# Weights of the up projection in raw buffers only, and both weight layouts as parts of two tiles

## The chip, the core and the metric

The kernel runs on one core of one Trainium2 chip. Time is device time of one execution in microseconds (us), less is better; a figure for a kernel is the median of its runs. A core has five engines with instruction streams of their own: TensorE (PE in the profile, with its weight loads shown apart as PEld), VectorE (DVE), ScalarE (ACT), GpSimd (POOL) and SyncE (SP). Each works through its stream in order and waits on semaphores for the others. In this kernel SP issues the loads of weights, POOL issues most other transfers, and DVE and ACT prepare operands and move results out of the accumulators.

## What is computed

One layer of a decoder on 512 rows of width 2048, in 32-bit floats. Attention of two kinds comes first; the change touches the second half, a gated feed-forward block with a causal convolution of width 3:

```python
def conv_ffn(h, w_up, w_conv, b_conv, w_down):
    S = h.shape[1]
    u = h @ w_up
    up = jnp.pad(u, ((0, 0), (CONV_W - 1, 0), (0, 0)))
    conv = b_conv
    for j in range(CONV_W):
        conv = conv + w_conv[j] * up[:, j:j + S]
    gate, val = jnp.split(conv, 2, axis=-1)
    return (jax.nn.silu(gate) * val) @ w_down
...
        h = rms_norm(x, g_ffn[l]) * (1.0 + sc_f) + sh_f
        x = x + gt_f * conv_ffn(h, w_up[l], w_conv[l], b_conv[l], w_down[l])
```

`w_up` is 2048 x 11264 and `w_down` is 5632 x 2048. Both products take most of the second half of the time.

## The kernel before

**Exact products from split operands.** TensorE multiplies in a shorter format, so every operand is split: `hi` is the value rounded to that format (made by ACT, line 130) and `lo` is what is left (made by DVE, line 131, which needs `hi`). A product is three matmuls: hi by hi (line 1082), hi by lo (1083) and lo by hi (1084).

**Seven products in place of eight.** `seven` (line 947) multiplies a 2x2 block of weights by a 2x2 block of activations in the Strassen-Winograd way. A `Pair` is two blocks of 128 output columns. It has four weight blocks L11, L21, L22 and L12, and seven *steps*, in the order p1, p7, p6, p2, p5, p4, p3. Each step has a *preparation* (the function of that name: load blocks, add or subtract blocks on DVE in `comb`, split the result in `hilo`), then K x 3 matmuls of 256 columns, then an *evacuation* (e1 to e3: the bank is copied by ACT at line 987 or added to a slot by DVE at line 993). For the up projection K is 8, so a step has 24 matmuls and a pair 168; there are 40 pairs, 280 steps and 6,720 matmuls. The sums are

- p1: load L11 and L21; split L11
- p7: S3 = L21 - L11; split S3; load L22
- p6: L21 = L21 + L22, then L11 = L21 - L11; split L11; load L12
- p2: split L12
- p5: split L21; L12 = L12 - L11; L11 and L21 are free
- p4: split L22; L22 is free
- p3: split L12; L12 is free

`run` (line 1073) writes for step q first the preparation of step q + AHEAD (2 for the up projection, 3 for the down projection), then its matmuls, then its evacuation. A scheduler then orders each engine's stream by its own simulation of the program, so an instruction may stand earlier on its engine than it was written.

**Two kinds of storage.** *Raw buffers* hold loaded weights: five of 1104 floats per partition, taken from the left of the queue `rawq` and put back on its right. Three pairs of `hi_b`, `lo_b` hold the split weights and are used in turn (`cnt["wt"]` modulo 3), so the split for step q must wait until the matmuls of step q - 3 are done. *Slots* are 81 tiles of 512 floats for everything else: activations, sums, evacuated results. In the up projection `slots=True` (line 1534, the first 34 pairs) puts S3 and L12, 1024 floats each, into two slots each. Each operation on them is then two instructions of 512 columns (`cuts`, `part`), and the load of L12 is two transfers of 256 KB. The last six pairs use raw buffers for all blocks, in queue order: S3 then takes the *oldest* free raw buffer.

**The turn.** The down projection has blocks of 640 or 768 floats and other buffers: seven raw and four split pairs of 768. `weight_bufs` closes the pool of tiles and opens another in the same memory. `turn` does this, and writes the first three preparations of the down projection, behind the matmuls of the very last up step (line 1085).

**Around it.** After each pair of the up projection `ffn_out` does the convolution (ACT line 1379, DVE lines 1380 and 1381), the gate (ACT 1460, DVE 1463) and, in `f_out`, sums on DVE (1401 to 1404) and stores of the result to DRAM through POOL (1397, 1406). The down projection reads these back through POOL (`load_tile`, line 1482: two transfers, one for each half of a slot) and splits them (`split_tile`); `ahead` starts this in the last 56 up steps, as far as slots are free. Stores that add to the output run through POOL too (1553). Ahead of the 40 pairs, `up_group(0)` does the first 512 gate and value columns by plain products (`lin_fm`, splits at lines 122 and 123 in the same `hi_b`, `lo_b`).

Of the kernel before, what the change touches and what calls it, by code (L numbers as in the profile page):

```python
# [10 lines left out]
F32 = mybir.dt.float32  # L11
F32R = mybir.dt.float32r  # L12
# [6 lines left out]
P = 128  # L19
T = 512  # L20
# [11 lines left out]
def trunk_layer_kernel(  # L32
# [68 lines left out]
    weight_bufs(5, 3, 1104)  # L101
    ctx.callback(wpool.close)
    cnt = {"wt": 0, "half": 0, "at": 0}
# [165 lines left out]
    for ks in (range(0, 7), range(7, 14), range(14, KD)):  # L269
# [4 lines left out]
        for k in ks:  # L274
            t = get()
# [653 lines left out]
    class Pair:  # L929


        def __init__(self, rs, load, fin, K=KH, scale=None, slots=False):
            self.rs, self.load, self.fin, self.K, self.scale, self.slots = rs, load, fin, K, scale, slots

    def seven(work, pairs_of_banks, hook=None, AHEAD=2):
        def pair_steps(n, p):
# [18 lines left out]

            def part(t, lo, hi):

                for b, x, y in t:
                    if x <= lo and hi <= y:
                        return b[:, lo - x:hi - x]  # L960

            def cuts(*ts):
                return [(x, y) for _, x, y in max(ts, key=len)]

            def load(blk, slots=False):
                t = new(slots)
                for b, x, y in t:
                    SP.dma_start(b[:, :y - x], p.load(blk)[:, x:y])
                return t

            def hilo(t):
                i = cnt["wt"] % len(hi_b)
                cnt["wt"] += 1
                hi, lo = hi_b[i][:, :W], lo_b[i][:, :W]
                for x, y in cuts(t):
                    split(hi[:, x:y], lo[:, x:y], part(t, x, y))
                return hi, lo

            def comb(o, a, b, op):
                for x, y in cuts(o, a, b):  # L980
                    V.tensor_tensor(part(o, x, y), part(a, x, y), part(b, x, y), op)  # L981
# [18 lines left out]
            def p7():  # L1000
                s3 = new(p.slots)
                comb(s3, L[21], L[11], ALU.subtract)
                r = hilo(s3)
                done(s3)
                L[22] = load(3)
                return r

            def p6():
# [3 lines left out]
                L[12] = load(2, p.slots)  # L1012
# [56 lines left out]
        def start():  # L1069
            for q in range(AHEAD):  # L1070
                prepare(q)

        def run(then=None):
            for q, (_, o, r, ev, first, K) in enumerate(steps):
                prepare(q + AHEAD)
                wh, wl = ready.pop(q)
# [8 lines left out]
                if then and q == len(steps) - 1:  # L1085
                    then()
# [447 lines left out]
    work = [Pair(rs, lambda blk, i=i: w_ups[i, blk], ffn_out(i), slots=i < NF_ - 10) for i in range(NF_ - 4)]  # L1534
# [26 lines left out]
    up_start, up_run = seven(work, all_banks, up_hook)  # L1561
# [73 lines left out]
```

## Time and profile before

| | |
|---|---|
| median of three runs | 2711.05 us (2710.53, 2711.05, 2716.68) |
| the profiled execution | 2708.11 us, of which the span of its instructions is 2706.3 us |
| PE busy | 2613.8 us, 97% of the span, 17,200 matmuls |
| DVE, ACT, POOL busy | 2180.2 us (81%), 1281.9 us (47%), 363.6 us (13%) |
| moved | 464.33 MB, 172 GB/s on average |
| matmuls of lines 1082, 1083, 1084 | 3,920 each, 1108.2, 1101.6 and 1094.3 us busy |
| splits by line 130 (ACT) and 131 (DVE) of raw buffers | 458 each, 424.6 and 482.1 us busy |
| loads of `w_ups` | 126 of 512 KB into raw buffers, 68 of 256 KB into slots |

How to read it: consecutive matmuls overlap in the records (a matmul of 256 columns is shown with 0.28 us, and the next begins about 0.12 us after it), so how fast PE goes is read from the number of matmuls in a stretch of time, not from its busy share. A view by *windows* gives for each engine the busy time and, in brackets, the count of instructions in a stretch, and the clock granted to PE as a share of full speed. A view of *waits* says which engine and line waited for which, with total us, number of times and the longest. A line of the *timeline* is start, duration, engine, line, operation, destination and sources; in square brackets is the idle time of the engine just before it, and what ended it. SPq is the queue of transfers that SP issues.

### The profile page before, as it was taken

How to read it: one execution, taken by the hardware profiler on the slowest of the kernel's cores; microseconds unless marked ns; L12 is line 12 of the kernel's file. 1: busy time of each engine (PE TensorE's matmuls, PEld its weight loads, DVE VectorE, ACT ScalarE, POOL GpSimd, SP SyncE). 2: the span in 40 equal slices, each digit the busy share in tenths (PEclk: the TensorE clock that was granted, in tenths of full speed). 3: DMA queues.
4: the chain of work that ended last, by engine and by line, in shares of the span. 5: the costliest groups of instructions: out<-in, count | busy, mean ns of one | idle time of the engine just before them, and what ended most of it. 6: DMA issues, size and time to landing. Idle time of an engine off the chain costs nothing.

```text
span 2706.3 us, 45437 instructions
## 1 busy us (share of the span) xinstructions
PE 2613.8 (97%) x17200; PEld 2345.9 (87%) x17200; DVE 2180.2 (81%) x3669; ACT 1281.9 (47%) x2069; POOL 363.6 (13%) x663
## 2 busy tenths in 40 slices
PE   6999999999999999999999999999999999999999
PEld 5787687778997767788789999999999988899999
DVE  7977976688878667983778888888889888778777
ACT  4333434334444455322545555555555555545454
POOL 1001011110032222110100000000001032413120
PEclk8999899999999999999999999999999999999999
DMA  9953136665585588962333343334334456767563
GB/s 340 339 160 98 33 112 213 196 217 164 195 265 158 164 260 283 332 231 94 133 128 114 124 139 115 127 114 141 127 110 148 131 178 181 188 163 192 138 204 116
DMA packets 220559, 464.33 MB, mean 172 GB/s; under 512 B 24330, under 2 KB 65700, under 8 KB 220340
## 3 DMA queue, kind: packets, MB, share of 16 engines
q1 hardware_dynamic: 175156, 344.93, 39.0%
q0 software_dynamic: 45152, 116.50, 15.0%
q8 instruction: 134, 2.20, 0.3%
q14 instruction: 85, 0.70, 0.1%
q10 hardware_dynamic: 32, 0.01, 0.0%
HBM read 397.11 MB, written 64.23 MB: 170 GB/s over the span
## 4 chain that ended last, share of the span: by engine, by line
PE 53%; DVE 16%; issue 15%; DMA 13%; POOL 2%; ACT 1%; SPq 0%; DVEq 0%; POOLq 0%; ACTq 0%
PE bank L134 9%; PE bank L135 9%; PE bank L136 9%; PE bank L1082 7%; PE bank L1083 7%; PE bank L1084 7%; DVE wlo L131 6%; DMA raw<-in_w_ups 5%; DMA slot<-in_w_ada 2%; DMA raw<-in_w_down 2%; DVE raw L981 2%; DVE slot L981 1%; DVE slot L1380 1%; DMA raw<-in_w_in 1%; DVE slot L1381 1%
## 5 line engine op out<-in xcount | busy, mean ns | idle before, releaser
L1082 PE MATMUL bank<-slot,whi 128*128 128x256 f32 x3920 | 1108.2, 283 | 44.8 <-DVE slot L991 13.1
L1083 PE MATMUL bank<-slot,whi 128*128 128x256 f32 x3920 | 1101.6, 282 | 0.4 <-DVE slot L131 0.4
L1084 PE MATMUL bank<-slot,wlo 128*128 128x256 f32 x3920 | 1094.3, 282 | 5.7 <-DVE wlo L131 5.6
L1082 PEld LDWEIGHTS bank<-slot,whi 128*128 128x128 f32 x3920 | 743.2, 190 | 58.3 <-DVE slot L993 16.5
L1084 PEld LDWEIGHTS bank<-slot,wlo 128*128 128x128 f32 x3920 | 737.2, 189 | 8.6 <-DVE wlo L131 8.3
L1083 PEld LDWEIGHTS bank<-slot,whi 128*128 128x128 f32 x3920 | 742.2, 189 | 0.9 <-DVE slot L131 0.6
L130 ACT ACTIVATE whi<-raw 128x1024 fp32r<-128x1024 f32 (+2 forms) x458 | 424.6, 928 | 463.8 <-PE bank L1083 352.0
L131 DVE TENSOR_TENSOR wlo<-raw,whi 128x1024 fp32r<-128x1024 f32 (+2 forms) x458 | 482.1, 1058 | 54.3 <-ACT whi L130 53.0
L122 ACT ACTIVATE whi<-raw 128x1024 fp32r<-128x1024 f32 (+4 forms) x182 | 187.2, 1031 | 392.0 <-PE bank L136 198.9
L123 DVE TENSOR_TENSOR wlo<-raw,whi 128x1024 fp32r<-128x1024 f32 (+4 forms) x182 | 216.5, 1191 | 147.7 <-ACT whi L122 146.3
L981 DVE TENSOR_TENSOR raw<-raw,raw 128x1024 f32<-128x1024 f32 (+2 forms) x252 | 265.2, 1053 | 68.7 <-DMA raw<-in_w_down 47.5
L135 PE MATMUL bank<-wlo,slot 128*128 128x512 f32 (+2 forms) x768 | 297.0, 387 | 0.9 <-DVE wlo L123 0.9
L134 PE MATMUL bank<-whi,slot 128*128 128x512 f32 (+2 forms) x768 | 289.6, 390 | 6.8 <-ACT slot L401 4.3
L136 PE MATMUL bank<-whi,slot 128*128 128x512 f32 (+2 forms) x768 | 292.0, 384 | 0.0
L135 PE MATMUL bank<-slot,whi 128*128 128x512 f32 (+1 forms) x656 | 263.0, 401 | 1.2 <-DVE slot L703 1.1
L134 PE MATMUL bank<-slot,whi 128*128 128x512 f32 (+1 forms) x656 | 260.8, 403 | 3.1 <-ACT slot L1370 2.3
L136 PE MATMUL bank<-slot,wlo 128*128 128x512 f32 (+1 forms) x656 | 257.5, 401 | 0.4 <-DVE wlo L123 0.4
L134 PEld LDWEIGHTS bank<-whi,slot 128*128 128x128 f32 x768 | 145.8, 190 | 38.1 <-ACT slot L401 4.4
L135 PEld LDWEIGHTS bank<-wlo,slot 128*128 128x128 f32 x768 | 146.2, 190 | 29.4 <-DVE wlo L123 1.4
L739 DVE SCALAR_TENSOR_TENSOR slot<-slot,c_act,slot 128x512 f32<-128x512 f32 x203 | 149.6, 749 | 25.3 <-DMA slot<-in_w_ada 24.3
L136 PEld LDWEIGHTS bank<-whi,slot 128*128 128x128 f32 x768 | 144.7, 189 | 28.4 <-issue 0.3
L130 ACT ACTIVATE whi<-slot 128x512 fp32r<-128x512 f32 x204 | 128.0, 628 | 82.0 <-PE bank L1083 60.7
(294 smaller groups left out, 3115.0 us busy)
## 6 DMA issues: line engine op xcount, KB each, us to landing
slot<-in_w_ada SPq DMA_DIRECT2D x344, 256.0 KB, 5.6
raw<-in_w_ups SPq DMA_DIRECT2D x126, 512.0 KB, 4.3
raw<-in_w_in SPq DMA_DIRECT2D x50, 512.0 KB, 3.6
raw<-in_w_down SPq DMA_DIRECT2D x64, 384.0 KB, 5.1
raw<-in_w_down SPq DMA_DIRECT2D x64, 320.0 KB, 4.2
slot<-f POOLq DMA_DIRECT2D x154, 128.0 KB, 3.8
slot<-in_w_ups SPq DMA_DIRECT2D x68, 256.0 KB, 2.7
f<-slot POOLq DMA_DIRECT2D x66, 256.0 KB, 5.3
```

The lines of the kernel that those rows point to most:

```text
L122: A.activation(hi, raw[:, :w], AF.Copy)
L123: V.tensor_tensor(lo, raw[:, :w], r32(hi), ALU.subtract)
L130: A.activation(dst_hi, src, AF.Copy)
L131: V.tensor_tensor(dst_lo, src, r32(dst_hi), ALU.subtract)
L134: PE.matmul(o, lh, rh, start=first, stop=False)
L135: PE.matmul(o, lh, rl, start=False, stop=False)
L136: PE.matmul(o, ll, rh, start=False, stop=last)
L739: V.scalar_tensor_tensor(acc, ts[i], c_act[:, k:k + 1], acc, op0=ALU.mult, op1=ALU.add)
L981: V.tensor_tensor(part(o, x, y), part(a, x, y), part(b, x, y), op)
L1082: PE.matmul(o, wh[:, ks], rh, start=first and k == 0, stop=False, skip_group_check=True)
L1083: PE.matmul(o, wh[:, ks], rl, start=False, stop=False, skip_group_check=True)
L1084: PE.matmul(o, wl[:, ks], rh, start=False, stop=last, skip_group_check=True)
```

## The change

The whole diff is below. It makes one tile `wraw` of 5 x 1104 floats and one tile `whl` of 6 x 1104; `weight_bufs` now only cuts them anew, and hands out the raw parts in the order in which the parts of the old layout that they overlap come free. The option `slots` and the helpers for blocks in two pieces go away: all 40 pairs of the up projection hold L11, L21, L22 and L12 in raw buffers. S3 takes the newest free raw buffer (`rawq.pop()`) and gives it back at once, and L22 and L12 take the oldest. `turn` is called in every step with the number of steps left: two steps ahead of the end it cuts the buffers anew and prepares the first down step, in the last step the second, and the third follows behind the up projection. `cnt["wt"]` is set to 2 ahead of the up projection, so that the split pair 0 is the one due at the new cut.

```diff
     bank = [psum.tile([P, T], F32, name=f"bank{i}") for i in range(8)]
-    wpool = ExitStack()
-    hi_b, lo_b, rawq = [], [], deque()
+    WR, WS = 5 * 1104, 6 * 1104
+    wraw = pool.tile([P, WR], F32, name="raw")
+    whl = pool.tile([P, WS], F32R, name="whl")
+    hi_b, lo_b, rawq, raw_at = [], [], deque(), []
+    cnt = {"wt": 0, "half": 0, "at": 0}
 
     def weight_bufs(nr, nh, w):
 
-        wpool.close()
-        wp = wpool.enter_context(tc.tile_pool(name=f"w{w}", bufs=1))
+
+        assert nr * w <= WR and 2 * nh * w <= WS and len(rawq) == len(raw_at)
+        age = [[i for i, t in enumerate(rawq) if t is b[0]][0] for b in raw_at]
+
+        def freed(x):
+            return max([a for a, (_, lo, hi) in zip(age, raw_at) if lo < x + w and x < hi], default=0)
+
+        raw_at[:] = [(wraw[:, i * w:(i + 1) * w], i * w, (i + 1) * w) for i in sorted(range(nr), key=lambda i: freed(i * w))]
         rawq.clear()
-        rawq.extend([wp.tile([P, w], F32, name=f"raw{w}_{i}") for i in range(nr)])
-        hi_b[:] = [wp.tile([P, w], F32R, name=f"whi{w}_{i}") for i in range(nh)]
-        lo_b[:] = [wp.tile([P, w], F32R, name=f"wlo{w}_{i}") for i in range(nh)]
+        rawq.extend(b[0] for b in raw_at)
+        hi_b[:] = [whl[:, 2 * i * w:(2 * i + 1) * w] for i in range(nh)]
+        lo_b[:] = [whl[:, (2 * i + 1) * w:(2 * i + 2) * w] for i in range(nh)]
+        cnt["wt"] = 0
 
     weight_bufs(5, 3, 1104)
-    ctx.callback(wpool.close)
-    cnt = {"wt": 0, "half": 0, "at": 0}
...
-            def new(slots=False):
-                if slots:
-                    return [(get(), 0, T), (get(), T, W)]
-                return [(rawq.popleft(), 0, W)]
-
             def done(t):
-                if len(t) == 1:
-                    rawq.append(t[0][0])
-                else:
-                    put(*(x[0] for x in t))
-
-            def part(t, lo, hi):
-
-                for b, x, y in t:
-                    if x <= lo and hi <= y:
-                        return b[:, lo - x:hi - x]
-
-            def cuts(*ts):
-                return [(x, y) for _, x, y in max(ts, key=len)]
-
-            def load(blk, slots=False):
-                t = new(slots)
-                for b, x, y in t:
-                    SP.dma_start(b[:, :y - x], p.load(blk)[:, x:y])
+                rawq.append(t)
+
+            def load(blk):
+                t = rawq.popleft()
+                SP.dma_start(t[:, :W], p.load(blk))
                 return t
 
             def hilo(t):
                 i = cnt["wt"] % len(hi_b)
                 cnt["wt"] += 1
                 hi, lo = hi_b[i][:, :W], lo_b[i][:, :W]
-                for x, y in cuts(t):
-                    split(hi[:, x:y], lo[:, x:y], part(t, x, y))
+                split(hi, lo, t[:, :W])
                 return hi, lo
 
             def comb(o, a, b, op):
-                for x, y in cuts(o, a, b):
-                    V.tensor_tensor(part(o, x, y), part(a, x, y), part(b, x, y), op)
+                V.tensor_tensor(o[:, :W], a[:, :W], b[:, :W], op)
...
             def p7():
-                s3 = new(p.slots)
+
+                s3 = rawq.pop()
                 comb(s3, L[21], L[11], ALU.subtract)
                 r = hilo(s3)
                 done(s3)
...
-                L[12] = load(2, p.slots)
+                L[12] = load(2)
                 return r
...
-        def start():
-            for q in range(AHEAD):
+        def start(*qs):
+            for q in qs or range(AHEAD):
                 prepare(q)
 
         def run(then=None):
             for q, (_, o, r, ev, first, K) in enumerate(steps):
                 prepare(q + AHEAD)
+                if then:
+                    then(q - len(steps))
                 wh, wl = ready.pop(q)
...
-                if then and q == len(steps) - 1:
-                    then()
                 ev()
...
-    work = [Pair(rs, lambda blk, i=i: w_ups[i, blk], ffn_out(i), slots=i < NF_ - 10) for i in range(NF_ - 4)]
+    work_up = [Pair(rs, lambda blk, i=i: w_ups[i, blk], ffn_out(i)) for i in range(NF_ - 4)]
...
-    def turn():
-        weight_bufs(7, 4, 768)
-        down_start()
-
+    def turn(q):
+
+
+        if q == -2:
+            assert cnt["wt"] % 3 == 0
+            weight_bufs(7, 4, 768)
+        if q >= -2:
+            down_start(q + 2)
+
+    cnt["wt"] = 3 - len(work_up) * 7 % 3
     up_start()
     up_run(turn)
+    down_start(2)
     down_run()
```

More of the change, by code (lines that the diff above doesn't have):

```diff
@@ L929, in trunk_layer_kernel, with __init__ @@
     class Pair:
-        def __init__(self, rs, load, fin, K=KH, scale=None, slots=False):
-            self.rs, self.load, self.fin, self.K, self.scale, self.slots = rs, load, fin, K, scale, slots
+        def __init__(self, rs, load, fin, K=KH, scale=None):
+            self.rs, self.load, self.fin, self.K, self.scale = rs, load, fin, K, scale
     def seven(work, pairs_of_banks, hook=None, AHEAD=2):
@@ L1559, in down_pair @@
                     scale=tuple(mod[:, 80 + n:81 + n] for n in ns))
-    up_start, up_run = seven(work, all_banks, up_hook)
+    up_start, up_run = seven(work_up, all_banks, up_hook)
     work = [down_pair(c, j) for c in range(len(DH)) for j in range(KD // 2)]
```

## The prediction, made before the changed kernel was run

> **What bounds the kernel now.** I read the page first, then windows along the up projection, then who waits for whom in two stretches of it, then the timeline of one pair and of the turn.
>
> ```profile
> span 2706.3 us, 45437 instructions
> PE 2613.8 (97%) x17200; PEld 2345.9 (87%) x17200; DVE 2180.2 (81%) x3669; ACT 1281.9 (47%) x2069; POOL 363.6 (13%) x663
> PE 53%; DVE 16%; issue 15%; DMA 13%; POOL 2%; ACT 1%; SPq 0%; DVEq 0%; POOLq 0%; ACTq 0%
> ```
>
> PE is busy 97% of the span, yet only 53% of the chain of waits is PE. Since matmuls overlap in the records, the busy share hides small gaps, so I count matmuls in windows.
>
> ```profile
> core 0: us, PE busy (x) PEld busy (x) DVE busy (x) ACT busy (x) POOL busy (x), PEclk, DMA share, GB/s
> 1402.50:1500.00 97.50, 93.45 (x784) 92.59 (x783) 88.71 (x132) 51.05 (x79) 8.64 (x16) 1.00 0.39 136
> 1500.00:2083.00 583.00, 572.22 (x4782) 566.33 (x4782) 514.43 (x741) 311.83 (x485) 35.53 (x66) 1.00 0.38 128
> 2083.00:2200.00 117.00, 116.68 (x988) 116.48 (x988) 104.95 (x128) 63.20 (x86) 8.62 (x16) 1.00 0.41 128
> ...
> 2223.00:2227.00 4.00, 0.00 (x0) 0.00 (x0) 1.28 (x2) 0.69 (x2) 2.64 (x5) 0.65 0.95 305
> 2227.00:2231.00 4.00, 3.83 (x16) 3.54 (x17) 3.92 (x7) 2.56 (x5) 0.53 (x1) 0.50 0.87 328
> 2231.00:2240.00 9.00, 6.42 (x47) 5.60 (x47) 9.00 (x15) 6.81 (x12) 5.86 (x12) 1.00 0.72 221
> ```
>
> The matmuls of the pairs begin at 1402.5. Until 2083 the pairs hold S3 and L12 in slots; from 2083 to 2200 run the last six, which hold all in raw buffers. So this trace has both schemes in it. A matmul takes 583/4782 = 0.1219 us in the first stretch and 117/988 = 0.1184 us in the second. PE's best 50 us show what is left after that:
>
> ```profile
> 2150.00:2200.00 50.00, 50.00 (x426) 50.00 (x425) 43.54 (x52) 26.52 (x35) 3.77 (x7) 1.00 0.47 148
> ```
>
> 50/426 = 0.1174 us. Who waits, in the stretch with slots (DVE's and PE's waits, two answers), and then in the stretch without:
>
> ```profile
> DVE slot L981 <- DMA raw<-in_w_ups: 55.4, 27, 4.2
> DVE raw L981 <- DMA raw<-in_w_ups: 5.4, 15, 0.8
> ...
> PE bank L1082 <- DVE slot L993: 7.6, 19, 0.8
> PE bank L1084 <- DVE wlo L131: 2.8, 3, 1.3
> ```
>
> ```profile
> DVE raw L981 <- DMA raw<-in_w_ups: 7.3, 9, 2.1
> ...
> PE bank L1082 <- DVE slot L993: 0.3, 1, 0.3
> ```
>
> With slots, DVE stands 55.4 us at S3 (line 981 into a slot) for a load, in order, and behind it stand the additions of line 993 that empty a bank that PE wants to write. One such case:
>
> ```profile
> 1869.61 1.23 DVE L981 TENSOR_TENSOR raw<-raw,raw 128x1024 f32<-128x1024 f32 x1 [0.81 <-DMA raw<-in_w_ups]
> 1870.75 0.69 DVE L131 TENSOR_TENSOR wlo<-slot,whi 128x512 fp32r<-128x512 f32 x1
> 1871.36 0.42 DVE L993 TENSOR_TENSOR slot<-bank,slot 128x256 f32<-128x256 f32 x1
> ...
> 1871.83 0.39 PE L1082 MATMUL bank<-slot,whi 128*128 128x256 f32 x1 [0.49 <-DVE slot L993]
> ```
>
> **The change part by part.** *Blocks in raw buffers.* Per slot pair, S3 (one sum, one split) and L12 (one sum, two splits) lose two-piece form: five DVE and three ACT operations go from two instructions to one.
>
> ```profile
> L131 DVE TENSOR_TENSOR wlo<-raw,whi 128x1024 fp32r<-128x1024 f32 x114 | 139.1, 1220 | 1.7 <-ACT whi L130 1.0 <-PE bank L1083 0.7
> L131 DVE TENSOR_TENSOR wlo<-slot,whi 128x512 fp32r<-128x512 f32 x172 | 117.8, 685 | 0.3 <-ACT whi L130 0.3
> L981 DVE TENSOR_TENSOR slot<-raw,raw 128x512 f32<-128x512 f32 x56 | 36.3, 689 | 55.4 <-DMA raw<-in_w_ups 55.4
> ```
>
> By these durations each merge saves 2 x 685 - 1220 = 150 ns. But instructions overlap: the row at 1870.75 is followed after 0.61 us though it lasts 0.69, and the one at 1869.61 after 1.14 though it lasts 1.23. So a merge is worth 2 x 0.61 - 1.14 = 0.08 us, 0.4 us of DVE a pair of 20.5 us. (The Trainium skill, VectorE: DVE Perf Modes, The DRAIN you can't avoid, says that the next operation does not start until the pipe is empty, save one that is not held; by the first the merge would be worth the full 0.15 us. The starts above, 0.08 us ahead of the end, decide for the second.) DVE is not what sets the end here, so this alone I cost at nothing on PE; the waits matter.
>
> The load of L12 becomes one transfer of 512 KB for two of 256 KB: the same bytes, one issue fewer on SP, which has only these loads. When can the loads start? In the changed order L11 takes the buffer that S3 of the last pair had (free early), L21 the one freed by p5's subtraction, L22 the one freed by p5's split, L12 the one freed by p4's split. S3 needs L21 and the buffer that p3's split has just left. In one pair of the trace:
>
> ```profile
> 1844.48 0.69 DVE L981 TENSOR_TENSOR slot<-slot,raw 128x512 f32<-128x512 f32 x1
> 1845.09 1.22 DVE L131 TENSOR_TENSOR wlo<-raw,whi 128x1024 fp32r<-128x1024 f32 x1
> ...
> 1847.29 1.22 DVE L131 TENSOR_TENSOR wlo<-raw,whi 128x1024 fp32r<-128x1024 f32 x1
> ...
> 1850.81 0.68 DVE L131 TENSOR_TENSOR wlo<-slot,whi 128x512 fp32r<-128x512 f32 x1
> 1852.67 1.29 DVE L981 TENSOR_TENSOR slot<-raw,raw 128x512 f32<-128x512 f32 x2 [1.18 <-DMA raw<-in_w_ups]
> ```
>
> ```profile
> raw<-in_w_ups SPq DMA_DIRECT2D x84, 512.0 KB, 4.7
> ...
> DMA to landing us min/median/max: 2.5/3.6/7.5
> ```
>
> p5's subtraction ends at 1845.2, so L21 lands at 1849.9 by the median 4.7 of this stretch. p3's split ends at 1851.5, so S3 would wait for DVE's own work and not for the load, with 1.6 us to spare. L22 (from 1846.3) is wanted only after S3, L12 (from 1848.5) three steps on. Today the scheduler puts S3 a pair early, because its slots are free, and there it meets a load that has just been issued. So I take the rate of the last six pairs: 4782 x 0.1184 = 566.3, a gain of 16.7 us; bounds: half of it (8), and PE's best rate, 583 - 4782 x 0.1174 = 21.6.
>
> *The first pairs and the reset of the counter.* 784 matmuls in 97.5 us could be done in 92.8, but part of the 4.7 us lies in the start, where DVE and ACT still work off the plain products. 182 splits at line 122 and 56 of the gate's pairs have been counted by then, so the next split pair would be 238 mod 3 = 1; the change sets it to 2. p1 then waits for the last plain group but one, and p7's split for the last group, at 1402.7.
>
> ```profile
> 1402.74 1.06 ACT L130 ACTIVATE whi<-raw 128x1024 fp32r<-128x1024 f32 x1 [0.41 <-PE bank L135]
> ...
> 1404.53 1.22 DVE L131 TENSOR_TENSOR wlo<-raw,whi 128x1024 fp32r<-128x1024 f32 x1
> ```
>
> p7 gets the place that p6's split has here and is done at 1405.7; PE wants it after 24 matmuls, at 1402.7 + 2.8 = 1405.5. So 0.2 us, at most a split (1.1 + 1.2). Net gain of this part 1 us, bounds -2 and 4.7. In the last six pairs only the choice of buffers changes: 0, at best 117 - 988 x 0.1174 = 1.
>
> *The turn.* Now the first down load waits until the last up matmul has read its weights:
>
> ```profile
> 2221.51 27.23 SPq L968 DMA_DIRECT2D raw<-in_w_down  x11
> ...
> 2226.31 0.74 ACT L130 ACTIVATE whi<-raw 128x640 fp32r<-128x640 f32 x1 [3.57 <-DMA raw<-in_w_down]
> ...
> 2227.10 0.58 PE L1082 MATMUL bank<-slot,whi 128*128 128x256 f32 x1 [5.62 <-ACT whi L130]
> ```
>
> After the change the first loads wait for raw parts that are free steps earlier, and the first two splits for split pairs 0 and 1, read last by the third and second step from the end: 2 x 2.8 and 2.8 us ahead of the end. So the wait of 5.62 us goes. But from 2227 to 2240 DVE is busy 3.92 of 4 and 9.00 of 9 us (splits of what the down projection reads back, and the last convolution), and PE does 63 matmuls where 111 fit. This stall is next in line: DVE's work is not less, it only begins sooner, so the gain is DVE's idle time in the hole, 4 - 1.28 = 2.7 us, and some tenths around it. I take 3.3; bounds 0 (the loads meet POOL's at 0.95 of the DMA engines) and 5.6 + 2.1 = 7.7, which adds the half clock of 2227 to 2231, where 16 matmuls did what 34 could. The clock fell to 0.65 and 0.50 behind the hole and was 1.00 after 2231. (The Trainium skill, TensorE: Matmul & The Clock Gate, The HAM clock gate, has an idle window of about 3.4 us halve the clock; the trace agrees, and by this rule a hole under 3.4 us would keep full clock, and the sum would be 2.1 us better if DVE let PE use it.)
>
> The seven down buffers and four split pairs are as large as before; after the turn I expect the same, at 0.
>
> **Sum**, against the profiled execution: 2708.1 - 16.7 - 1.0 - 0 - 3.3 = 2687.1. The median of the runs is 2.9 above that execution, so 2690.
>
> **The rivals.** *Half:* PE waits for line 993 because DVE is full (514 of 583 us), not because of the loads; then 8 of the 16.7 and 2 at the turn: 2701. Against it: the last six pairs have DVE just as full (105 of 117 us) and PE waits 0.3 us. *All of it:* 21.6 + 2 + 1 + 7.7 = 32.3, so 2679; DVE's full stretch at the turn speaks against. *Given back:* PE reaches the down projection earlier, but what it reads back through POOL does not come earlier, and the down phase stretches to the old end, 2709. For it: POOL's loads are on the path after the turn. Against: what frees slots for them are up steps, which move too. *Slower, late loads:* five raw buffers with none to spare. At S3 DVE now stands 55.4 us in 28 pairs, 2.0 a pair. With 6.3 us between p5's subtraction and S3, a landing beyond 6.3 + 2.0 = 8.3 us makes it worse; at 9.3 in every pair, 40 x 1.0 = 40 us, some 2748. The longest landing in the stretch is 7.5, so it needs loads that delay each other. *Not what it says:* if parts of one tile were ordered like the whole, each load would wait for all readers, 4.7 us exposed in some 160 loads, beyond 3000 us. Against it, halves of one slot are loaded back to back, half a microsecond apart, though a landing takes 2.4 to 3.8:
>
> ```profile
> 2202.42 1.59 POOL L1482 DMA_DIRECT2D slot<-f  x3
> ...
> DMA to landing us min/median/max: 2.4/3.1/3.8
> ```
>
> **How the numbers follow.** Forecast 0.60, half 0.17, all of it 0.07, given back 0.05, late loads 0.08, one tile 0.03. About 0.3% (8 us, below 2703) can be told from no change. Faster: 0.60 + 0.07 + 0.11 of the half case = 0.78; same: 0.06 of it + 0.05 = 0.11; slower 0.08 + 0.03 = 0.11. The range runs from 2678, just beyond all of it, to 2706, which takes in the half case and leaves out giving back and slower, 0.16.
>
> **What would show it.** Right: no line 981 into a slot; DVE's waits for the loads of the up projection at some 10 us for its whole length; 0.1184 us a matmul from start to end; the first load of the down projection before the last up matmul, no hole above 2 us there, the clock at 1.00, and DVE still full for 10 us. Wrong: new waits of line 981 for loads in raw buffers; the same rate with fewer DVE waits (half); or a slower down projection.

## The result and the profile after

The changed kernel takes 2672.2 us (median of 4 runs, 2669.1 to 2673.3) where the kernel before took 2713.9 us beside it (4 runs, 2710.5 to 2719.0): ratio 0.9843, 95% interval 0.9823 to 0.9863. The direction was forecast; the gain is about twice the forecast, and 2672.2 lies below the range of 2678 to 2706.

The page of the changed kernel: its span, the engines, the group of the sums (busy us, mean ns, idle us before them and what ended most of it), and the loads of the up projection (count, size, median us from issue to landing):

```profile
span 2670.9 us, 45030 instructions
PE 2610.9 (98%) x17200; PEld 2351.5 (88%) x17200; DVE 2178.5 (82%) x3499; ACT 1268.3 (47%) x1967; POOL 362.3 (14%) x663
...
L968 DVE TENSOR_TENSOR raw<-raw 128x1024 f32<-128x1024 f32 (+2 forms) x320 | 347.1, 1085 | 6.3 <-DMA raw<-in_w_ups 3.4
...
raw<-in_w_ups SPq DMA_DIRECT2D x160, 512.0 KB, 4.9
```

DVE has 170 instructions less and about the same busy time (2178.5 against 2180.2 us). The merging was costed at nothing on PE and at 0.4 us of DVE a pair, 13.6 us in 34 pairs; DVE's busy time in the first 34 pairs fell by only 1.9 us (619.9 to 618.0). The sums wait 3.4 us in all for loads of the up projection. The line numbers have moved. The matmuls are lines 1072 to 1074 now, the splits 138 (ACT) and 139 (DVE), the sums 968, the evacuations 974 and 972 (ACT) and 980 and 978 (DVE), the loads 957.

To see where the time went, I cut each trace at matmuls. Of the 11,760 matmuls of the three lines, in order of their starts, the first 1,344 belong to attention, the next 5,712 to the first 34 pairs, 1,008 to the last six, and 3,696 to the down projection. Each entry is the difference of two starts, in us:

| | span | start of the pairs | first 34 pairs | last six | turn | down projection |
|---|---|---|---|---|---|---|
| before | 2706.3 | 1402.7 | 698.1 | 120.4 | 5.9 | 474.8 |
| after | 2670.9 | 1406.0 | 679.4 | 125.0 | 0.1 | 455.8 |
| difference | -35.4 | +3.3 | -18.7 | +4.6 | -5.8 | -18.9 |

The rest of the difference, 0.1, is rounding and what follows the last matmul. The +3.3 can't be put down to the change: in the other kernels below the pairs start anywhere from 1400.5 to 1409.2. Nor is it shown to be no part of it. The 1,344 matmuls of attention are eight pairs that go through `seven` and `p7` too, so the change touches them as well: S3 takes the newest buffer there. From the first to the last of them it is 170.2 us before and 174.8 after; the four kernels here with the oldest buffer in these pairs have 170.2 to 172.7, the eleven with the newest 172.3 to 174.8.

Windows of the changed kernel (columns as before): the middle of the first 34 pairs, the last six, and the turn.

```profile
core 0: us, PE busy (x) PEld busy (x) DVE busy (x) ACT busy (x) POOL busy (x), PEclk, DMA share, GB/s
...
1500.00:1750.00 250.00, 250.00 (x2113) 250.00 (x2112) 226.52 (x264) 132.60 (x176) 13.47 (x25) 1.00 0.39 131
...
2085.00:2210.00 125.00, 120.34 (x1010) 119.53 (x1008) 111.77 (x138) 68.62 (x98) 24.03 (x45) 1.00 0.47 153
2210.00:2214.00 4.00, 4.00 (x36) 3.95 (x34) 4.00 (x8) 3.52 (x7) 3.42 (x7) 1.00 0.89 263
2214.00:2220.00 6.00, 3.32 (x24) 2.76 (x23) 6.00 (x10) 4.44 (x8) 2.66 (x6) 1.00 0.86 279
2220.00:2230.00 10.00, 8.44 (x69) 8.03 (x69) 10.00 (x20) 6.22 (x11) 4.92 (x9) 1.00 0.60 204
```

250/2113 is 0.1183 us a matmul, the forecast rate. At the turn there is no hole and the clock stays at 1.00, but DVE is full from 2210 to 2230 and PE does 129 matmuls where 169 would fit: the stall that was named as next in line is there. The transfers of SP at the turn begin 20 us ahead of the last up matmul (2210.4):

```profile
2190.31 45.75 SPq L957 DMA_DIRECT2D raw<-in_w_down  x14
```

The surprise is the down projection. Its waits in the kernel before (us in all, times, longest; DVE's, then PE's), from 2227 to 2702:

```profile
DVE raw L981 <- DMA raw<-in_w_down: 47.5, 26, 3.9
...
PE bank L1082 <- DVE slot L991: 13.1, 9, 3.1
```

and in the changed one, from 2210 to 2666:

```profile
DVE whl L139 <- ACT whl L138: 55.1, 64, 2.2
...
PE bank L1072 <- ACT slot L972: 5.5, 9, 1.3
PE bank L1074 <- DVE whl L139: 2.7, 4, 0.9
PE bank L1072 <- ACT whl L138: 2.3, 3, 1.6
```

DVE's 47.5 us of waits for loads are gone, and with them PE's 13.1 us for DVE's evacuations. One of those places in the kernel before:

```profile
2384.09 2.82 DVE L131 TENSOR_TENSOR wlo<-raw,whi 128x768 fp32r<-128x768 f32 x3
2389.19 0.96 DVE L981 TENSOR_TENSOR raw<-raw,raw 128x768 f32<-128x768 f32 x1 [2.29 <-DMA raw<-in_w_down]
2390.07 0.48 DVE L991 SCALAR_TENSOR_TENSOR slot<-bank,mod,slot 128x256 f32<-128x256 f32 x1
...
2390.60 0.38 PE L1082 MATMUL bank<-slot,whi 128*128 128x256 f32 x1 [0.99 <-DVE slot L991]
```

This is the picture that the prediction drew for the slots of the up projection, in the down projection, which has no slots: a sum waits for a load, the evacuation queues behind it, PE waits for the bank.

### The profile page after: what moved, and what is told of

Its sections match the earlier page's. It is cut to its first block, busy times and chain, and to the rows that moved or that the text cites. A ratio compares the mean times of both kernels' runs of the same rounds, so it can differ in the third digit from the quotient of the medians.

```text
span 2670.9 us, 45030 instructions
## 1 busy us (share of the span) xinstructions
PE 2610.9 (98%) x17200; PEld 2351.5 (88%) x17200; DVE 2178.5 (82%) x3499; ACT 1268.3 (47%) x1967; POOL 362.3 (14%) x663
## 5 line engine op out<-in xcount | busy, mean ns | idle before, releaser
L1072 PE MATMUL bank<-slot,whl 128*128 128x256 f32 x3920 | 1104.2, 283 | 20.5 <-ACT slot L972 5.5
L1073 PE MATMUL bank<-slot,whl 128*128 128x256 f32 x3920 | 1099.9, 282 | 0.2 <-DVE slot L139 0.2
L1074 PE MATMUL bank<-slot,whl 128*128 128x256 f32 x3920 | 1088.0, 281 | 6.3 <-DVE whl L139 6.3
L138 ACT ACTIVATE whl<-raw 128x1024 fp32r<-128x1024 f32 (+2 forms) x560 | 532.7, 953 | 617.2 <-PE bank L1073 404.3
L1072 PEld LDWEIGHTS bank<-slot,whl 128*128 128x128 f32 x3920 | 739.6, 189 | 27.7 <-ACT slot L972 8.2
L1073 PEld LDWEIGHTS bank<-slot,whl 128*128 128x128 f32 x3920 | 740.8, 189 | 0.6 <-DVE slot L139 0.5
L1074 PEld LDWEIGHTS bank<-slot,whl 128*128 128x128 f32 x3920 | 733.4, 189 | 7.5 <-DVE whl L139 7.5
L139 DVE TENSOR_TENSOR whl<-raw,whl 128x1024 fp32r<-128x1024 f32 (+2 forms) x560 | 605.7, 1087 | 121.2 <-ACT whl L138 118.9
L130 ACT ACTIVATE whl<-raw 128x1024 fp32r<-128x1024 f32 (+4 forms) x182 | 187.4, 1031 | 383.8 <-PE bank L144 201.9
L968 DVE TENSOR_TENSOR raw<-raw 128x1024 f32<-128x1024 f32 (+2 forms) x320 | 347.1, 1085 | 6.3 <-DMA raw<-in_w_ups 3.4
L131 DVE TENSOR_TENSOR whl<-raw,whl 128x1024 fp32r<-128x1024 f32 (+4 forms) x182 | 215.8, 1187 | 153.4 <-ACT whl L130 152.8
L143 PE MATMUL bank<-whl,slot 128*128 128x512 f32 (+2 forms) x768 | 297.1, 388 | 0.0
L142 PE MATMUL bank<-whl,slot 128*128 128x512 f32 (+2 forms) x768 | 290.3, 391 | 3.2 <-ACT slot L409 3.2
L144 PE MATMUL bank<-whl,slot 128*128 128x512 f32 (+2 forms) x768 | 292.9, 385 | 0.0
L142 PE MATMUL bank<-slot,whl 128*128 128x512 f32 (+1 forms) x656 | 261.7, 403 | 3.1 <-ACT slot L1358 2.3
L143 PE MATMUL bank<-slot,whl 128*128 128x512 f32 (+1 forms) x656 | 262.5, 400 | 1.4 <-DVE slot L711 1.3
L144 PE MATMUL bank<-slot,whl 128*128 128x512 f32 (+1 forms) x656 | 257.4, 401 | 0.4 <-DVE whl L131 0.4
L142 PEld LDWEIGHTS bank<-whl,slot 128*128 128x128 f32 x768 | 146.1, 190 | 33.4 <-ACT slot L409 3.3
L143 PEld LDWEIGHTS bank<-whl,slot 128*128 128x128 f32 x768 | 146.2, 190 | 28.9 <-issue 0.5
L144 PEld LDWEIGHTS bank<-whl,slot 128*128 128x128 f32 x768 | 144.7, 189 | 29.5 <-issue 0.5
```

What stands on the lines that cost most here:

```text
L130: A.activation(hi, raw[:, :w], AF.Copy)
L131: V.tensor_tensor(lo, raw[:, :w], r32(hi), ALU.subtract)
L138: A.activation(dst_hi, src, AF.Copy)
L139: V.tensor_tensor(dst_lo, src, r32(dst_hi), ALU.subtract)
L142: PE.matmul(o, lh, rh, start=first, stop=False)
L143: PE.matmul(o, lh, rl, start=False, stop=False)
```

## Experiments

Times are medians; each ratio is against runs of the kernel before, taken beside them on the same chip, with its 95% interval. The last columns are the phases as above, from the profiled execution.

| kernel | us | ratio | first 34 | last six | turn | down |
|---|---|---|---|---|---|---|
| after | 2672.2 | 0.9843 (0.9823 to 0.9863) | 679.4 | 125.0 | 0.1 | 455.8 |
| s3_newest_only | 2698.7 | 0.9942 (0.9927 to 0.9957) | 694.6 | 125.4 | 5.9 | 461.2 |
| down_s3_oldest | 2701.9 | 0.9958 (0.9944 to 0.9972) | 679.5 | 125.0 | 0.1 | 479.7 |
| layout_only | 2718.3 | 1.0020 (1.0007 to 1.0033) | 696.3 | 121.2 | 0.1 | 487.5 |
| late_turn | 2673.0 | 0.9845 (0.9829 to 0.9861) | 679.6 | 125.0 | 0.1 | 454.0 |
| with_slots | 2689.7 | 0.9902 (0.9882 to 0.9921) | 696.8 | 125.0 | 0.1 | 456.3 |
| no_slots_only | 2698.7 | 0.9940 (0.9915 to 0.9965) | 674.8 | 120.3 | 4.0 | 490.0 |
| up_s3_oldest | 2672.4 | 0.9838 (0.9816 to 0.9859) | 682.5 | 119.4 | 0.1 | 456.5 |
| hi_lo_apart | 2671.1 | 0.9832 (0.9812 to 0.9853) | 678.5 | 124.9 | 0.1 | 456.8 |
| six_down_raw | 2682.0 | 0.9891 (0.9876 to 0.9906) | 679.5 | 125.0 | 0.1 | 465.6 |
| down_oldest_held | 2687.0 | 0.9897 (0.9873 to 0.9921) | 679.7 | 125.8 | 0.1 | 470.4 |
| last_six_oldest | 2668.4 | 0.9838 (0.9823 to 0.9854) | 679.9 | 119.3 | 0.1 | 458.0 |
| own_pool | 2666.7 | 0.9838 (0.9820 to 0.9856) | 677.2 | 124.7 | 0.1 | 451.1 |
| last_six_oldest_own_pool | 2658.3 | 0.9805 (0.9790 to 0.9820) | 678.1 | 119.0 | 0.1 | 453.5 |

**Which part gives the gain of the down projection.** The kernel before with the newest raw buffer for S3 wherever S3 is in a raw buffer (the eight pairs of attention, the last six up pairs and the whole down projection):

```diff
-                s3 = new(p.slots)
+                s3 = new(True) if p.slots else [(rawq.pop(), 0, W)]
```

> The kernel before with one edit: where S3 lies in a raw buffer (last six up pairs, all of the down projection) it takes the newest free one. Before, the down projection takes 474.8 us from its first to its last matmul, after the change 455.8. Theory buffer (the choice for S3 lets the next loads start earlier): about 456 to 460 us for the down projection, its waits of DVE for loads of the down weights (47.5 us in all) gone, the whole about 17 us below the kernel before. Theory turn (the down projection gains because its first loads come early and stay ahead, or from the layout): 475 us, no change of the whole.

The down projection falls from 474.8 to 461.2, with the old layout and the old turn. And the reverse, the changed kernel with the oldest buffer in the down projection only:

```diff
-                s3 = rawq.pop()
+                s3 = rawq.pop() if p.K == KH else rawq.popleft()
```

> The changed kernel with one edit: in the down projection S3 takes the oldest free raw buffer again. Theory buffer: the down projection goes back from 455.8 to about 470 us, and DVE waits some 40 us for its loads; the whole 14 to 19 us above the changed kernel's 2672. Theory turn: it stays at 456, the whole at 2672.

It rises from 455.8 to 479.7 (the phases are those of the profiled execution, here the fastest of 7; the median is 29.7 us above the changed kernel's), and the waits of the kernel before are back (DVE's, then PE's, 2210 to 2666):

```profile
DVE raw L968 <- DMA raw<-in_w_down: 44.0, 25, 3.6
...
PE bank L1072 <- DVE slot L978: 15.5, 10, 2.9
```

So the choice of buffer alone is worth 13.6 us in the old kernel and 23.9 in the changed one, in the phase that the forecast left at 0. Part of the 23.9 is clock: by the granted clock in the traces PE has half clock for 17.1 us of the down projection in down_s3_oldest, for 7.4 in the kernel before and for none in the changed one. If a matmul takes twice as long then, that is at most some 8.5 us (an estimate). The rest of the change costs a little in this phase: with the oldest buffer it takes 4.9 us more in the changed kernel than before (479.7 to 474.8), for reasons that no run separates.

**The turn.** The kernel before with the two tiles and nothing else: slots, the oldest buffer and the turn written behind the last step stay.

```diff
-        wpool.close()
-        wp = wpool.enter_context(tc.tile_pool(name=f"w{w}", bufs=1))
...
+        raw_at[:] = [(wraw[:, i * w:(i + 1) * w], i * w, (i + 1) * w) for i in sorted(range(nr), key=lambda i: freed(i * w))]
...
+        hi_b[:] = [whl[:, 2 * i * w:(2 * i + 1) * w] for i in range(nh)]
+        lo_b[:] = [whl[:, (2 * i + 1) * w:(2 * i + 2) * w] for i in range(nh)]
```

> The kernel before with only the two tiles and their cutting anew; slots, S3 from the oldest raw buffer and the late turn stay. Both theories: the up projection stays at 818 us within 3. Theory buffer: the hole of 5.9 us shrinks by 0 to 5 us as the first loads no longer wait for the last matmul, the down projection stays at 470 to 475 us, the whole 0 to 6 us below the kernel before. Theory turn in its form with the layout: the down projection falls to about 456 us. It also shows whether the 3.3 us that the changed kernel is later at the first up matmul, and its 0.1184 in place of 0.1180 us between matmuls that wait for nothing, come from the layout.

And the changed kernel with the turn written behind the last step, as before:

```diff
-                if then:
-                    then(q - len(steps))
...
+                if then and q == len(steps) - 1:
+                    then()
...
-    down_start(2)
```

> The changed kernel with the turn put back behind the matmuls of the last up step, all three preparations there. Theory buffer: the hole ahead of the first down matmul returns in part (3 to 6 us; the loads still need not wait for PE, as raw parts are free), the rest of the down projection stays within 3 us of 455.8, the whole 3 to 8 us above 2672. Theory turn: the down projection returns to about 475 us, the whole about 25 us above.

The layout closes the hole by itself, 5.9 to 0.1. Where the turn is written does not matter: the phases agree with the changed kernel's to 2 us, and the 3 to 6 us of the hole that were forecast do not come back; the scheduler orders the streams in any case. But in layout_only the time is 0.2% longer than before, and the down projection, forecast at 470 to 475 us, takes 487.5. More than the hole's 5.8 us comes back there, with longer waits for loads (47.5 before; DVE from 2220 to 2700; line 988 is the sums there):

```profile
DVE raw L988 <- DMA raw<-in_w_down: 57.4, 28, 3.9
```

So in these runs closing the hole pays only with the newest buffer for S3.

**The up projection.** The changed kernel with the slots back in the first 34 pairs (the helpers of the old code, and S3 in a raw buffer still takes the newest):

```diff
+                s3 = new(True) if p.slots else [(rawq.pop(), 0, W)]
...
+                L[12] = load(2, p.slots)
...
+    work = [Pair(rs, lambda blk, i=i: w_ups[i, blk], ffn_out(i), slots=i < NF_ - 10) for i in range(NF_ - 4)]
```

> The changed kernel with S3 and L12 of the first 34 up pairs in slots again; the two tiles, the early turn, the counter and the newest raw buffer for S3 elsewhere stay. Theory slots (S3 computed a pair early stands for its load and holds up the evacuations): the first 34 pairs go from 679.4 back to 694 to 698 us, hole and down projection stay as in the changed kernel (0.1 and 454 to 461), the whole at 2687 to 2691. Rival (the up projection gains because of the newest buffer or the layout, not the slots): 680 us and 2672.

The kernel before without slots:

```diff
-    work = [Pair(rs, lambda blk, i=i: w_ups[i, blk], ffn_out(i), slots=i < NF_ - 10) for i in range(NF_ - 4)]
+    work = [Pair(rs, lambda blk, i=i: w_ups[i, blk], ffn_out(i), slots=False) for i in range(NF_ - 4)]
```

> The kernel before with one edit: all 40 up pairs keep S3 and L12 in raw buffers, S3 in the oldest one. Theory slots: the first 34 pairs at 678 to 682 us in place of 698.1, last six at 120.4, hole 5.9 and down projection at 475 as before; the whole 16 to 20 us below the kernel before. Rival (the newest buffer or the layout is what counts): 690 us or more, the whole within 8 us of the kernel before.

The changed kernel with the oldest buffer for S3 in the up projection (and in the eight pairs of attention, whose K is 8 too), the newest in the down projection:

```diff
-                s3 = rawq.pop()
+                s3 = rawq.popleft() if p.K == KH else rawq.pop()
```

> The changed kernel, but S3 takes the oldest free raw buffer in the up projection, the newest in the down projection. Theory slots: the first 34 pairs stay within 2 us of 679.4, as their gain came from the slots, not from the choice of buffer; the last six pairs go from 125.0 back to about 120.5 us, as in the two kernels that take the oldest there; the whole 2667 to 2669, below both kernels. Rival (the up projection needs the newest buffer too): the first 34 pairs at 690 or more.

In the changed kernel the slots are worth 696.8 - 679.4 = 17.4 us, the term of 16.7; in the kernel before, 698.1 - 674.8 = 23.3. But no_slots_only misses its forecast in the down projection, where nothing was changed: 490.0 us for 475, in an execution 6.2 us above the median of its runs. Half clock covers 23.0 us of it, and DVE waits longer for the loads (2204 to 2700):

```profile
DVE raw L981 <- DMA raw<-in_w_down: 60.4, 31, 4.3
```

So in this execution, with the oldest buffer, a good part of what the up projection gains is given back in the down projection.

In the changed kernel the newest buffer adds only 3.1 us to the first 34 pairs (682.5 to 679.4), though DVE's waits for loads differ much. With the oldest buffer, 1500 to 2083:

```profile
DVE raw L968 <- DMA raw<-in_w_ups: 43.5, 53, 2.1
```

With the newest, 1406 to 2085.5:

```profile
DVE raw L968 <- DMA raw<-in_w_ups: 2.8, 3, 1.2
```

Those 43.5 us are in 53 waits of 0.8 us, against 27 of 2.1 us with slots before (the row with 55.4): PE hardly notices the short ones. In no_slots_only, too, DVE waits 41.7 us for these loads, in 55 waits, and its 674.8 us are the shortest of all. One of the long waits, at S3 in the kernel before (DVE, then PE):

```profile
1770.39 1.29 DVE L981 TENSOR_TENSOR slot<-raw,raw 128x512 f32<-128x512 f32 x2 [1.87 <-DMA raw<-in_w_ups]
1771.60 0.42 DVE L993 TENSOR_TENSOR slot<-bank,slot 128x256 f32<-128x256 f32 x1
...
1772.07 0.39 PE L1082 MATMUL bank<-slot,whi 128*128 128x256 f32 x1 [0.77 <-DVE slot L993]
```

And in the last six pairs the newest buffer costs 5.6 us (119.4 to 125.0). The two and the other phases nearly cancel: up_s3_oldest takes 2672.4 us like the changed kernel, and not the 2667 to 2669 that were forecast.

**The last six pairs.** PE waits for ACT four times there (2085.5 to 2210.3):

```profile
PE bank L1072 <- ACT slot L974: 2.6, 2, 1.3
PE bank L1072 <- ACT whl L138: 2.1, 2, 1.0
```

The first of them, ACT's timeline and then PE's:

```profile
2130.89 1.06 ACT L138 ACTIVATE whl<-raw 128x1024 fp32r<-128x1024 f32 x1 [1.77 <-PE bank L1073]
2131.85 0.37 ACT L974 ACTIVATE slot<-bank 128x256 f32<-128x256 f32 x1
...
2132.27 0.38 PE L1072 MATMUL bank<-slot,whl 128*128 128x256 f32 x1 [1.30 <-ACT slot L974]
```

A split stands ahead of an evacuation in ACT's stream, it waits for PE itself, and PE wants the evacuated bank. The oldest buffer for S3 in those six pairs alone:

```diff
-                s3 = rawq.pop()
+                s3 = rawq.popleft() if p.K == KH and n >= 34 else rawq.pop()
```

> The changed kernel, but S3 takes the oldest raw buffer in the last six up pairs alone. If the choices add up: first 34 pairs at 679.4, last six at 119.4 to 121 (125.0 in the changed kernel), hole 0.1, down projection 454 to 457; the whole about 2667, 5 below the changed kernel. If the last six are slow because of what comes ahead of them: 125 and 2672.

The last six fall to 119.3. The time is 3.8 us less than the changed kernel's, but the two ratios overlap; the phase is clear, the total alone would not be. How the buffer of S3 leads to that order on ACT was not followed further.

**Why the oldest buffer is slow.** In the compiled stream of DVE, with buffer numbers, the kernel before has this (output, then inputs; other rows left out):

```
L981 raw768_2 <- raw768_1,raw768_0   S3 of a pair
L981 raw768_6 <- raw768_6,raw768_3   p5's subtraction of the pair before
...
L131 wlo768_2 <- raw768_2            S3 split, 9 rows behind the subtraction
...
L981 raw768_2 <- raw768_6,raw768_5   S3 of the next pair
L981 raw768_4 <- raw768_4,raw768_0   p5's subtraction of the pair before
```

Buffer 2 holds S3 of every pair: given back, it is always the oldest when S3 is wanted, so six buffers hold loads. And because it is always free, the scheduler can put S3 ahead of the pair before's p5, where its loads have just been issued. In s3_newest_only S3 goes into buffers 0, 4, 1 and 5 in turn, the one that p3's split has just left, and stands behind that split. Two causes, then: a buffer less, and S3 too early. First, the buffer: the changed kernel, newest, with six down buffers.

```diff
-            weight_bufs(7, 4, 768)
+            weight_bufs(6, 4, 768)
```

> The changed kernel with six raw buffers in the down projection in place of seven. Theory spare buffer (with the oldest buffer for S3 one buffer goes back and forth for S3 alone and six hold loads; with the newest all seven hold loads): six with the newest are as good as seven with the oldest, so the down projection takes 476 to 484 us as in that run (479.7), DVE waits some 45 us for its loads, the whole 2694 to 2704. Rival (the newest buffer helps in another way, for instance because S3 reuses memory just written, and the number of buffers has slack): 456 to 462 us, the whole 2672 to 2678.

The down projection takes 465.6, between the two forecasts (476 to 484, and 456 to 462), so a buffer less costs 9.8 of the 23.9, and DVE's waits for loads come back in part (2210 to 2680; some 45 us were forecast):

```profile
DVE raw L968 <- DMA raw<-in_w_down: 14.5, 11, 3.2
```

Then the place: down_s3_oldest, with S3's sum kept behind p3's split of the pair before in DVE's stream (`p3_lo` is the list of those splits).

```diff
-                comb(s3, L[21], L[11], ALU.subtract)
+                with tc.issue_after(p3_lo[-1].ins) if p3_lo and p.K != KH else nullcontext():
+                    comb(s3, L[21], L[11], ALU.subtract)
```

> The changed kernel with the oldest free buffer for S3 in the down projection (as in down_s3_oldest), and there S3's sum may be issued on VectorE only behind p3's split of the pair before. Six buffers hold loads, as in six_down_raw; what differs from down_s3_oldest is only that S3 can't run ahead. Theory (about 10 us of the 23.9 are the buffer that S3 keeps for itself, the other 14 are S3 issued a pair early, where VectorE stands for a load just issued): hole and down projection together fall from 479.8 to about 466, VectorE's waits for down loads from 45.2 us to about 15, time about 2688 (ratio about 0.990). Rival (the buffer that is kept back and the rotation are all of it; the place of S3 in the order is a symptom): down stays at 477 to 480 and the time at 2699 to 2702 (ratio about 0.995).

The down projection falls from 479.7 to 470.4, and the median from 2701.9 to 2687.0. Forecast were 466 and 2688 if the place counts, 477 to 480 and 2699 to 2702 if it doesn't. So the place is worth 9.3 us. These two parts hold clock as well: half clock covers 17.1 us in down_s3_oldest, 6.8 in six_down_raw and 3.4 in down_oldest_held. The last 4.8 of the 23.9 are not settled: DVE still waits 25.3 us for loads, where 15 were forecast and six_down_raw has 14.5. PE waits less for DVE's evacuations than in down_s3_oldest (line 980 here, 2.9 us for 15.5) but more for splits (9.6 for 1.6) and for ACT's evacuations (line 974 here, 8.4 for 5.5), and one reading is that S3's split now comes late (2210 to 2680):

```profile
PE bank L1078 <- DVE whl L139: 9.6, 8, 2.0
PE bank L1076 <- ACT slot L974: 8.4, 11, 1.5
PE bank L1076 <- ACT whl L138: 3.0, 4, 1.2
PE bank L1076 <- DVE slot L980: 2.9, 3, 1.6
```

**The interval of the matmuls.** In stretches without waits a matmul followed the last after 0.1180 us in the up projection before, and after 0.1184 in the changed kernel (mean of all intervals up to 0.13 us). On 6,720 matmuls that is 2.7 us. In layout_only it is 0.1183, so it comes with the two tiles. Is it that hi and lo parts alternate in the tile? All hi parts ahead of all lo parts; the new cut then overwrites split weights of the last up step ahead of its matmuls, and the amount of work is the same:

```diff
-        hi_b[:] = [whl[:, 2 * i * w:(2 * i + 1) * w] for i in range(nh)]
-        lo_b[:] = [whl[:, (2 * i + 1) * w:(2 * i + 2) * w] for i in range(nh)]
+        hi_b[:] = [whl[:, i * w:(i + 1) * w] for i in range(nh)]
+        lo_b[:] = [whl[:, (nh + i) * w:(nh + i + 1) * w] for i in range(nh)]
```

> The changed kernel with all hi parts of the tile of split weights ahead of all lo parts, and not in turns. Where a matmul waits for nothing its interval in the up projection was 0.1180 us in the kernels with tiles of their own and 0.1184 in those with the two tiles. If the order of hi and lo in memory does this: 0.1180 again, 2 to 3 us less. If it is where the tiles lie, or something else: 0.1184 and 2672.

0.1183: nothing. Is it where tiles lie in memory? The same two tiles in a pool of their own, opened at that place:

```diff
-    wraw = pool.tile([P, WR], F32, name="raw")
-    whl = pool.tile([P, WS], F32R, name="whl")
+    wpool = ctx.enter_context(tc.tile_pool(name="w", bufs=1))
+    wraw = wpool.tile([P, WR], F32, name="raw")
+    whl = wpool.tile([P, WS], F32R, name="whl")
```

> The changed kernel with its two weight tiles in a pool of their own, as the weight tiles of the kernel before, so that they lie elsewhere in memory. If the place sets the interval of a matmul that waits for nothing: 0.1180 us in the up projection, 2 to 3 us less than 2672. If not: 0.1184 and 2672.

Yes: the up projection is back at 0.1180 and the down projection goes from 0.1185 to 0.1170 (0.1189 in the kernel before). But the edit moves more than the two tiles. In the compiled programs `raw` goes from byte 4,224 of a partition to byte 179,936, behind everything else, and with that the slots, which hold the activations, go from byte 53,888 on to byte 5,312 on. So the weights, the activations or their distance may be what counts. The intervals and the phases show the gain; the ratios of the two kernels overlap. The same 250 us as above, and 2500 to 2560, where the changed kernel does 499 matmuls:

```profile
1500.00:1750.00 250.00, 250.00 (x2121) 250.00 (x2120) 228.03 (x265) 132.97 (x176) 12.89 (x24) 1.00 0.39 130
...
2500.00:2560.00 60.00, 59.84 (x505) 59.10 (x504) 47.91 (x64) 31.31 (x51) 14.60 (x23) 1.00 0.67 175
```

**Both together.** The pool of own_pool and the line of last_six_oldest:

```diff
+    wpool = ctx.enter_context(tc.tile_pool(name="w", bufs=1))
...
+                s3 = rawq.popleft() if p.K == KH and n >= 34 else rawq.pop()
```

> Both edits together: if both help and add up, about 2665; if the place does nothing, 2667 as with the other edit alone.

```profile
span 2655.8 us, 45030 instructions
```

2658.3 us is 13.9 below the changed kernel, and the two ratio intervals do not touch. It is also 7 below the forecast: of the 15.1 us between the two spans 5.5 lie ahead of the pairs, where the kernels scatter by 8.7 us. This is the fastest version found.

## Why the prediction fell short

- *Blocks in raw buffers, -16.7; first pairs, -1.0.* Right: the first 34 pairs fell by 18.7, and the slots alone account for 17.4. The mechanism was right in the main: S3 a pair early stood for its load, and PE for what was behind it. But of PE's 19 waits for line 993 in the stretch with slots only 9 come behind such a wait of S3, and 9 behind one of a sum into a raw buffer. The waits of DVE for loads are at 3.4 us in the whole up projection where 10 were foreseen, but that they go was not needed: no_slots_only keeps 41.7 us of short ones, and PE has no wait in that stretch. The case that the prediction shows at 1869.61 is a sum into a raw buffer, from the row of 5.4 us, and not S3; a case of S3 is the one at 1770.39 above. That the rate came out at the forecast 0.1184 so closely is partly luck: with its old tiles the kernel reaches 23.3 without slots, and the two tiles lengthen every matmul's interval by 0.0004 us, 2.7 us in the up projection, a term that the prediction did not have.
- *Last six, "only the choice of buffers changes: 0", at best 1.* Wrong, +4.6. With the newest buffer a split comes ahead of an evacuation on ACT, and PE waits for that; with the oldest it doesn't. The bound was made from PE's best rate, on the gain's side alone.
- *The turn, -3.3 of 0 to 7.7.* The hole is gone (5.8), and the stall of DVE next in line is there. The reason holds in half: it is the layout, not the earlier place in the code, and the hole's time is not kept with the oldest buffer (layout_only).
- *"after the turn I expect the same, at 0".* This is the step that failed: -18.9. "The seven down buffers and four split pairs are as large as before" is true, but `p7` is shared: by attention's eight pairs, the up projection and the down projection. The prediction counted the queue order of the up projection step by step and did not ask the same of the down projection, whose 47.5 us of waits at line 981 stood in the trace of before. "Today the scheduler puts S3 a pair early, because its slots are free" was said of the slots; the raw buffer that the old queue order always gave to S3 was just such a slot. The choice of buffer is worth 23.9 us there by down_s3_oldest; the rest of the change takes 4.9 back.
- *The sum.* By phases, the forecast of -21.0 lacked 18.9 in the down projection, was 1.0 short in the first 34 pairs and 2.5 at the turn, and had 4.6 too much in the last six; with the start's +3.3 this makes the -35.4 of the spans to 0.1. The medians differ by 41.7, as the profiled execution of before was 5.8 under the median of the later runs.
- *Rivals.* None came true. *All of it* had 2679, but for a faster up projection; *half* needed a rate between 0.1184 and 0.1219; *given back* fell, as the down projection gained, but with the oldest buffer the down projection does stretch, in no_slots_only by 15.2 us and in layout_only by 12.7, and what grows there are DVE's waits for weights (47.5 to 60.4 and 57.4), while ACT waits at most 4.5 us for what POOL reads back; *late loads* and *one tile* needed waits at the sums, which are at 3.4 us.

## What to carry to other kernels

Before you cost a changed line at 0, list every caller of it (here there were three), and look in the waits of each caller's stretch for the line: a wait there is what the change can take away. A buffer that a queue hands to the same short-lived value each time is a private buffer; it takes one from the loads, and it lets the scheduler place that value so early that an engine which works in order stands at a load just issued. Here the early start of a phase was worth nothing until the buffers of that phase could use it.

## What the runs showed of the hardware

**Where tiles lie in memory changes the pace of the matmuls.** With as many instructions of each engine 0.1184 us became 0.1180 in the up projection, and 0.1185 became 0.1170 in the down projection. Why is open: no run moved one tile alone, and own_pool moved weights and activations at once.

**Half clock can follow a short pause.** In down_s3_oldest PE stands from one start to the next for 2.54 us at 2326.7, and then:

```profile
2326.70:2329.30 2.60, 0.34 (x4) 0.14 (x2) 2.60 (x5) 1.42 (x2) 0.80 (x2) 1.00 1.02 377
2329.30:2331.30 2.00, 2.00 (x11) 2.00 (x12) 2.00 (x4) 1.26 (x2) 1.45 (x4) 0.60 1.00 353
2331.30:2333.30 2.00, 2.00 (x12) 2.00 (x11) 2.00 (x4) 1.03 (x2) 1.94 (x4) 0.55 0.77 262
2333.30:2336.00 2.70, 2.70 (x25) 2.70 (x24) 2.70 (x5) 0.34 (x1) 2.24 (x6) 1.00 0.78 238
```

23 matmuls in 4 us where 34 fit. In the kernel before, a pause of 3.40 us had no such effect:

```profile
2594.40:2597.80 3.40, 0.28 (x4) 0.07 (x2) 1.30 (x3) 0.38 (x1) 1.23 (x3) 1.00 1.02 391
2597.80:2599.80 2.00, 2.00 (x17) 2.00 (x18) 2.00 (x4) 0.00 (x0) 0.56 (x2) 1.00 1.04 398
```

So a length of pause alone does not decide: in down_s3_oldest half clock also follows a pause of 2.12 us at 2456.1, and none follows one of 2.33 us at 2256.8. (The Trainium skill, TensorE: Matmul & The Clock Gate, The HAM clock gate, has the clock halved after at least one idle window of about 3.4 us, in windows that run on by themselves; the first of these rows differs from that, since 2.54 us holds no such window, and the measurement decides.) In the changed kernel the longest time between two starts of these matmuls from the pairs on is 1.84 us and the clock stays at 1.00, so part of what the down projection gained is clock. That length is not safe either: in hi_lo_apart the longest pause at the turn is 1.84 us too, and half clock follows it at 2230.4.
